# Moving mLSTM queries and keys into the seven-product stage of a hybrid decoder block, and DeltaNet key and value blocks in front of it

## The chip, the cores and the metric

One core of a Trainium2 chip runs the whole layer as one program. The metric is the device time of that program in microseconds (us), lower is better. A core has TensorE (PE in the profile; its weight loads are PEld), VectorE (DVE), ScalarE (ACT), GpSimd (POOL) and SyncE (SP), each of which works through its own list of instructions in order and waits on semaphores of the others. DMAs are issued from the lists of SP, ACT and POOL.

## What is computed

One decoder layer on 512 tokens, all in float32. A normalised input `u` (512 x 2048) is projected by one wide matrix, the columns go to two token mixers, and both results pass through one output matrix, sigmoid gates and a residual.

```python
def _hybrid_layer(h, norm_w, w_in, ...):
    u = _rmsnorm(h, norm_w)
    proj = jnp.matmul(u, w_in)
    (ml_q, ml_k, ml_v, ml_o, ml_z, ml_i, ml_f,
     dn_qkv, dn_z, dn_b, dn_a, gate_a, gate_b) = jnp.split(proj, idx, axis=-1)
    h_a = _mlstm_chunkwise(heads(ml_q), heads(ml_k), heads(ml_v), i_pre, logf)   # 8 heads
    h_a = merge(_rmsnorm(h_a)) * ml_norm_w * sigmoid(ml_o) * silu(ml_z)
    qkv = _causal_conv_silu(dn_qkv, dn_conv_w)          # 4 taps along the tokens, per channel
    dq, dk, dv = split(qkv)                             # 16 heads of 128 channels each
    h_b = _gated_delta_chunkwise(_l2norm(dq), _l2norm(dk), dv, beta, g)
    h_b = merge(_rmsnorm(h_b, dn_norm_w)) * silu(dn_z)
    return sigmoid(gate_a) * (h_a @ w_out[:2048]) + sigmoid(gate_b) * (h_b @ w_out[2048:])
```

The mLSTM has 8 heads with queries and keys of 128 channels (1024 columns of each in `w_in`); the DeltaNet has 16 heads of 128 channels for each of query, key and value.

## The kernel before

**Products.** Every float32 product is made of three TensorE products on values split in a high and a low part (`wh`/`wl` of the weights, `uh`/`ul` of the input): high by high, high by low, low by high. ACT makes the high part (`split_hi`, L140), DVE the low part (`split_lo`, L143). The order of TensorE's list is the order of the program text; the lists of the other engines are set by a scheduler that follows priorities (`urgent`, `high_priority`) and ties (`behind`, which puts an instruction after the newest split on an engine).

**Two ways to project.** `proj_cm` (L246) projects 256 columns straight: 16 row tiles x 2 column halves x 3 products = 96 matmuls of 128 x 512, and its result has channels on partitions and tokens along the row. Its weights come as tiles of 2 row tiles x 256 columns, four loads ahead (`load_raw`, a plan that lists every tile of the run) and three splits ahead. `seven_stage` (L480) projects two groups of 512 columns at once with a two-by-two scheme that needs seven block products where the straight way needs eight: 336 matmuls of 128 x 512 for 1024 columns, against 384. It costs extra sums on DVE (L519, L520, L538 on weights; L632 on results). A block has half A (8 stages of 4 products) and half B (8 stages of 3 products); the list `SEVEN` names the blocks, and each kind has a *sink* that takes the four results of a group off PSUM: `z` (gates of the mLSTM), `s` (gate of the DeltaNet), `q` (mLSTM queries and keys, turned to channels-first and written to DRAM), `v`, `g`.

**Stages.** (1) Front: the input is normalised, turned and split, while four `proj_cm` blocks run: queries and keys of mLSTM heads 0 to 3 (`QKFIRST = 2`), which `spill` writes to DRAM (`qk_d`). (2) The seven-product stage: 13 blocks; one of them is `q`, for heads 4 to 7. (3) Mixers: eight units (`dn_unit`), each for two DeltaNet heads. A unit runs three `proj_cm` blocks, key, value, query, and the rest of the work of several units and of the mLSTM heads is laid between their matmuls. (4) The output projection: three straight blocks, two seven-product blocks, one last straight block.

**Steps.** Work beside a projection is written as generators. `tick` (L219) is called after every six large matmuls (a *step*); a generator does a piece, says how many steps to wait, and goes on. So a unit of three `proj_cm` blocks has 48 steps, and the mixers have 384. For a unit, `conv_silu` and `silu_end` make convolution and SiLU (a scaled copy on ACT, three multiply-adds on DVE, tanh on ACT, one more on DVE), `turn` transposes 32 x 32 blocks on DVE and goes through DRAM for the rest. `dn_front_k` makes the products of the keys (`pk`), and solves small triangular systems on DVE (L964, L966) whose result comes back through DRAM as `tt` and is turned as `tn` (L982). `dn_back` (products `p1` to `p4`) starts 25 steps after the query block and needs `tn`. `dn_chain` runs through four chunks of tokens for each head: products `pr`, `pw`, `pst`, `po`, two steps apart, with one short DVE or ACT instruction between each (`r` L1082, `w` L1090, `st` L1100). `dn_front_q` makes `pqk` (L990), 9 steps after the query block. `ml_head` does the same for an mLSTM head (`psc`, `pnum`, `pcs`); `HEADS` lists the step at which each begins. All these short products share three PSUM buffers (`psw`) and the chains two (`pso`).

## Time and profile before

| | |
|---|---|
| time, median of 3 runs (lowest to highest) | 2144.73 us (2144.39 to 2144.76) |
| the profiled execution, its own time | 2143.23 us |
| its span in the profile | 2141.5 us |

The stages in the profiled execution (busy times of the engines inside each stretch, in us):

| stretch from the span's start | stage | length | PE | DVE | ACT | POOL |
|---|---|---|---|---|---|---|
| 0 to 124.6 | front | 124.6 | 107.93 | 89.10 | 59.45 | 5.15 |
| 124.6 to 1114.8 | seven-product stage, 13 blocks | 990.2 | 990.20 | 799.69 | 459.25 | 77.41 |
| 1114.8 to 1800.2 | mixers, 8 units | 685.4 | 685.10 | 557.43 | 383.61 | 276.39 |
| 1800.2 to 2141.5 | output projection | 341.3 | 330.28 | 261.77 | 155.34 | 92.17 |

How to read it: matmuls are pipelined, so one that takes 0.39 us on the page starts 0.23 us after the one before it; what a matmul costs is the distance between two starts, or the length of a stage divided by its matmuls. A busy PE means that the next matmul was always ready.

### The profile page before, as it was taken

The page shows a single profiled execution, that of the slowest core. Times are in us where ns is not written, and L with a number is a line of the kernel's source. Part 1 is how long each engine was busy: PE and PEld are TensorE (multiplying, and loading weights), DVE is VectorE, ACT ScalarE, POOL GpSimd, SP SyncE. Part 2 cuts the span into 40 slices and gives each one's busy share as a digit, 9 for nine tenths or more (in the row PEclk, how much of TensorE's full clock was granted, in tenths as well). Part 3 has the DMA queues.
Part 4 walks back from the last instruction along what each step waited for, and adds up shares of the span by engine and source line. Part 5 has one row for each costly group of instructions (what it writes and reads, how often), then busy time and mean ns, then how long its engine had stood idle before and what let it go on. Part 6 is the DMA issues. An engine that isn't in the chain of part 4 may idle for free.

```text
span 2141.5 us, 32018 instructions
## 1 busy us (share of the span) xinstructions
PE 2113.5 (99%) x10544; PEld 1752.6 (82%) x10544; DVE 1708.0 (80%) x2981; ACT 1057.6 (49%) x2066; POOL 451.1 (21%) x667
## 2 busy tenths in 40 slices
PE   6999999999999999999999999999999999999998
PEld 5888888888888888888888888888888888887886
DVE  5888888788788778777766887888878878569887
ACT  5444454445444444444445546456465464345345
POOL 0000000000004000000003335344343363233211
PEclk9999999999999999999999999999999999999999
DMA  5355676667677767766766867777686677778895
GB/s 162 119 192 190 212 217 198 220 199 224 206 234 237 245 196 226 240 209 212 253 205 165 208 166 180 183 180 192 182 211 173 171 189 224 196 223 287 245 302 225
DMA packets 447144, 444.21 MB, mean 207 GB/s; under 512 B 197121, under 2 KB 303842, under 8 KB 446850
## 3 DMA queue, kind: packets, MB, share of 16 engines
q1 hardware_dynamic: 377618, 337.22, 53.9%
q0 software_dynamic: 24752, 72.90, 10.9%
q10 hardware_dynamic: 44608, 32.06, 4.8%
q8 instruction: 82, 1.34, 0.3%
q14 instruction: 84, 0.69, 0.1%
HBM read 348.66 MB, written 97.58 MB: 208 GB/s over the span
## 4 chain that ended last, share of the span: by engine, by line
PE 95%; DVE 2%; DMA 2%; issue 1%; SPq 0%; POOL 0%; ACT 0%; DVEq 0%; POOLq 0%; ACTq 0%
PE ps L578 18%; PE ps L580 18%; PE ps L579 18%; PE pj L257 10%; PE pj L259 9%; PE pj L258 9%; PE py L1407 2%; PE py L1409 2%; PE py L1408 2%; PE pk L915 1%; DMA wr<-in_w_out_dram 1%; PE pqk L990 1%; PE pw L1087 1%; PE pnum L1213 1%; PE po L1102 1%
## 5 line engine op out<-in xcount | busy, mean ns | idle before, releaser
L143 DVE TENSOR_TENSOR wl<-wr,wh 128x512 fp32r<-128x512 f32 (+1 forms) x522 | 444.3, 852 | 176.5 <-ACT wh L140 172.3
L140 ACT CAST wh<-wr 128x512 fp32r<-128x512 f32 (+1 forms) x522 | 373.9, 717 | 422.1 <-PE pj L258 218.5
L257 PE MATMUL pj<-uh,wh 128*128 128x512 f32 x896 | 375.8, 419 | 0.0
L259 PE MATMUL pj<-uh,wl 128*128 128x512 f32 x896 | 351.5, 392 | 0.0
L258 PE MATMUL pj<-ul,wh 128*128 128x512 f32 x896 | 349.8, 390 | 0.0
L578 PE MATMUL ps<-wh,uh 128*128 128x512 f32 x752 | 292.7, 389 | 0.8 <-DVE X L632 0.8
L579 PE MATMUL ps<-wl,uh 128*128 128x512 f32 x752 | 292.6, 389 | 0.0
L580 PE MATMUL ps<-wh,ul 128*128 128x512 f32 x752 | 292.6, 389 | 0.0
L140 ACT CAST wh<-t 128x1024 fp32r<-128x1024 f32 x120 | 126.3, 1053 | 301.7 <-PE ps L580 197.5
L533 POOL DMA_DIRECT2D t_d<-ts x104 | 56.6, 544 | 921.8 <-DVE ts L520 853.5
L579 PE MATMUL ps<-wl,suh 128*128 128x512 f32 x624 | 242.9, 389 | 0.0
L580 PE MATMUL ps<-wh,sul 128*128 128x512 f32 x624 | 242.8, 389 | 0.0
L578 PE MATMUL ps<-wh,suh 128*128 128x512 f32 x624 | 242.8, 389 | 0.0
L140 ACT CAST wh<-ts 128x512 fp32r<-128x512 f32 x240 | 147.9, 616 | 184.7 <-DVE ts L538 157.6
L143 DVE TENSOR_TENSOR wl<-t,wh 128x1024 fp32r<-128x1024 f32 x120 | 147.0, 1225 | 81.9 <-ACT wh L140 81.5
L259 PEld LDWEIGHTS pj<-uh,wl 128*128 128x128 f32 x896 | 168.3, 188 | 37.0
L257 PEld LDWEIGHTS pj<-uh,wh 128*128 128x128 f32 x896 | 169.2, 189 | 29.7
L258 PEld LDWEIGHTS pj<-ul,wh 128*128 128x128 f32 x896 | 169.3, 189 | 28.5
L143 DVE TENSOR_TENSOR wl<-ts,wh 128x512 fp32r<-128x512 f32 x240 | 164.9, 687 | 32.6 <-ACT wh L140 31.2
L578 PEld LDWEIGHTS ps<-wh,uh 128*128 128x128 f32 x752 | 141.2, 188 | 30.4 <-DVE X L632 1.2
L579 PEld LDWEIGHTS ps<-wl,uh 128*128 128x128 f32 x752 | 141.2, 188 | 29.5
L580 PEld LDWEIGHTS ps<-wh,ul 128*128 128x128 f32 x752 | 141.2, 188 | 29.2
(345 smaller groups left out, 3804.2 us busy)
## 6 DMA issues: line engine op xcount, KB each, us to landing
wr<-in_w_in_dram SPq DMA_DIRECT2D x744, 256.0 KB, 3.6
wr<-in_w_out_dram SPq DMA_DIRECT2D x138, 256.0 KB, 4.8
t_d<-ts POOLq DMA_DIRECT2D x104, 256.0 KB, 3.6
wr<-t_d SPq DMA_DIRECT2D x104, 256.0 KB, 3.7
xt<-in_x_dram SPq DMA_DIRECT2D x8, 512.0 KB, 7.2
tg_d<-X ACTq DMA_DIRECT2D x16, 256.0 KB, 4.8
tg_d<-to ACTq DMA_DIRECT2D x16, 256.0 KB, 4.6
v<-v_d SPq DMA_DIRECT2D x8, 512.0 KB, 5.6
```

The lines of the kernel that those rows point to most:

```text
L140: newest["A"] = A.copy(hi, src).ins
L143: newest["V"] = V.tensor_tensor(out=lo, in0=src, in1=hi.bitcast(F32), op=ALU.subtract).ins
L257: T.matmul(ps[j], hi[:, k, wsl], uh[:, kt, :], start=(kt == 0), stop=False)
L258: T.matmul(ps[j], hi[:, k, wsl], ul[:, kt, :], start=False, stop=False)
L259: T.matmul(ps[j], lo[:, k, wsl], uh[:, kt, :], start=False, stop=(kt == KT - 1))
L533: queue.dma_start(t2_d[b % 2, i], ts[:, 0, :])
L578: T.matmul(ps[t], ah, hi, start=(g == "A" and i == 0), stop=False, skip_group_check=True)
L579: T.matmul(ps[t], ah, lo, start=False, stop=False, skip_group_check=True)
L580: T.matmul(ps[t], al, hi, start=False, stop=(i == KH - 1), skip_group_check=True)
L1407: T.matmul(ps[c], uh[:, kt, tsl], hi, start=(kt == ks[0]), stop=False)
L1408: T.matmul(ps[c], uh[:, kt, tsl], lo, start=False, stop=False)
L1409: T.matmul(ps[c], ul[:, kt, tsl], hi, start=False, stop=(kt == ks[-1]))
```

## The change

- **Columns change places.** All mLSTM queries and keys now go through the seven-product stage: `SEVEN` has two `q` blocks (one before the `v` blocks, one behind them), 14 blocks in all. The front's four `proj_cm` blocks are now DeltaNet blocks: the keys of heads 0 and 1, and the values of heads 3 and 5, 7 and 9, 11 and 13 (`PRE` lists their channel tiles). The value blocks load two column groups of 128 that lie 256 apart (kind `w`), in two DMAs per tile.
- **They are finished beside the stage.** `spill` writes the raw results to `raw_d`. In each of the first eight blocks of the seven-product stage, at the last stage of half A, `before_mixers` starts for one channel tile: load it, convolution and SiLU (one ACT multiply, three DVE multiply-adds, an ACT tanh, a DVE multiply-add), a DVE transpose, and the write to `pre_d` (for keys also to `kc_d`), issued from ACT.
- **Units get shorter.** Unit 0 has no key block (32 steps); units 1 to 6 project only one value head (`proj_half`: 48 matmuls, 8 steps; weight tiles of 4 row tiles x 128 columns) and load the other from `pre_d` (`turned`); they have 40 steps. Unit 7 keeps 48. The mixers have 320 steps.
- **Times within them.** `HEADS` is closer together, `dn_back` starts 28 steps after the query block (25 before; 27 in unit 0, 29 in unit 7 as before), and `dn_front_k` waits 11 steps for the solved systems in units 1 to 6 (16 before). `ml_head` loads keys and queries of all heads from `qt_d` and `k_d`; the transposes for heads 0 to 3 are gone. `open_y` starts at step 150 (200 before).

```diff
-QKFIRST = 2
-HEADS = (1, 41, 85, 130, 178, 226, 274, 322)
+HEADS = (1, 37, 74, 111, 148, 186, 225, 264)
+PRE = (16, 17, 35, 37, 39, 41, 43, 45)
+VPRE = {(h - 33) // 2: i for i, h in enumerate(PRE) if h > 32}
...
-         + [("q", ML_Q + QKS, ML_K + QKS)]
+         + [("q", ML_Q, ML_K)]
          + [("v", ML_V + c, ML_V + c + NO) for c in range(0, D, 2 * NO)]
+         + [("q", ML_Q + NO, ML_K + NO)]
...
-    QK = [(a, b) for b in range(QKFIRST) for a in range(2)]
-    plan = [("i", (ML_Q, ML_K)[a] + b * NB, k) for a, b in QK for k in range(0, KT, KP)]
+    FRONT = [("i", DN_K)] + [("w", DN_V + (h - 32) * P) for h in PRE[2::2]]
+    plan = [(*f, k) for f in FRONT for k in range(0, KT, KP)]
...
-        for c in (DN_K, DN_V, DN_Q):
-            plan += [("i", c + p * NB, k) for k in range(0, KT, KP)]
+        for c in (DN_K, DN_V, DN_Q)[p == 0:]:
+            if c == DN_V and p in VPRE:
+                plan += [("h", c + p * NB, k) for k in range(0, KT, 2 * KP)]
+            else:
+                plan += [("i", c + p * NB, k) for k in range(0, KT, KP)]
...
+    def proj_half(col0):
+        ps = psj.tile([P, S], F32, tag="pj", name="pj")
+        for kt0 in range(0, KT, 2 * KP):
+            hi, lo = next_w("h", col0, kt0)
+            for k in range(2 * KP):
+                kt = kt0 + k
+                T.matmul(ps, hi[:, k, :], uh[:, kt, :], start=(kt == 0), stop=False)
+                T.matmul(ps, hi[:, k, :], ul[:, kt, :], start=False, stop=False)
+                T.matmul(ps, lo[:, k, :], uh[:, kt, :], start=False, stop=(kt == KT - 1))
+                if k % 2:
+                    tick()
+        return [ps]
...
             for n in range(N - 2):
+                if n == KH - 1 and beside:
+                    start(beside.pop(0))
                 prep_sums(n0 + n + 1)
...
+    def before_mixers(i):
+        raw = wp.tile([P, S], F32, tag="wr", name="pr0", bufs=NRAW)
+        with behind("S"):
+            nc.sync.dma_start(raw, raw_d[i])
+        yield 4
+        ct = PRE[i]
+        y = wp.tile([P, S], F32, tag="wr", name="py0", bufs=NRAW)
+        with behind("A"):
+            A.mul(y, raw, convc[:, 144 + ct:145 + ct])
+        for j in (2, 1, 0):
+            with behind("V"):
+                V.scalar_tensor_tensor(out=y[:, 3 - j:S], in0=raw[:, 0:S - 3 + j], ...)
+            yield 1
+        with behind("A"):
+            A.activation(raw, y, AF.Tanh)
+        yield 1
+        with behind("V"):
+            V.scalar_tensor_tensor(out=y, in0=raw, scalar=1.0, in1=y, op0=ALU.add, op1=ALU.mult)
+        yield 1
+        with behind("V"):
+            V.transpose(raw, y)
...
-        yield 16
+        yield 11 if hs[0] // 2 in VPRE else 16
...
+            else:
+                nc.sync.dma_start(kq[j][:, 0, :], kc_d[j])
+                start(turned(ke, j), 3 + j, front)
...
-        ps = proj_cm(DN_V + dcol)
+        ps = (proj_half if p in VPRE else proj_cm)(DN_V + dcol)
...
-        start(dn_back(hs, kq, u), 25 + 4 * last, by)
+        start(dn_back(hs, kq, u), 28 - (p == 0) + last, by)
```

**Where it stands in DVE's list.** Two places show the order. The first is DVE in the second block of the seven-product stage, just behind the last two result sums of half A. `X` is the sum buffer, `wr3` a raw weight tile, `ts` a weight sum, `wl` a low part. Before:

```order
L632 TENSOR_TENSOR X_517<-X_517,ps_1806 128x512
L632 TENSOR_TENSOR X_517<-X_517,ps_1807 128x512
L143 TENSOR_TENSOR wl_2198<-wr3_2117,wh_2197 128x1024
L538 TENSOR_TENSOR ts_2223<-wr3_2155 128x512
L143 TENSOR_TENSOR wl_2230<-wr3_2155,wh_2229 128x1024
L538 TENSOR_TENSOR ts_2255<-wr3_2201 128x512
L143 TENSOR_TENSOR wl_2226<-ts_2223,wh_2225 128x512
L143 TENSOR_TENSOR wl_2258<-ts_2255,wh_2257 128x512
L143 TENSOR_TENSOR wl_2262<-wr3_2201,wh_2261 128x1024
```

In the changed kernel, at the same place (its lines are numbered anew: L632 is now L661, L143 is L146, L538 is L565; `py0` and `pr0` are the tiles of `before_mixers`):

```order
L661 TENSOR_TENSOR X_523<-X_523,ps_1847 128x512
L661 TENSOR_TENSOR X_523<-X_523,ps_1848 128x512
L146 TENSOR_TENSOR wl_2241<-wr3_2158,wh_2240 128x1024
L565 TENSOR_TENSOR ts_2271<-wr3_2196 128x512
L822 SCALAR_TENSOR_TENSOR py0_2254<-pr0_2208,convc_85,py0_2254 128x511
L146 TENSOR_TENSOR wl_2278<-wr3_2196,wh_2277 128x1024
L565 TENSOR_TENSOR ts_2307<-wr3_2244 128x512
L822 SCALAR_TENSOR_TENSOR py0_2254<-pr0_2208,convc_85,py0_2254 128x510
L146 TENSOR_TENSOR wl_2274<-ts_2271,wh_2273 128x512
L822 SCALAR_TENSOR_TENSOR py0_2254<-pr0_2208,convc_85,py0_2254 128x509
L146 TENSOR_TENSOR wl_2310<-ts_2307,wh_2309 128x512
L146 TENSOR_TENSOR wl_2314<-wr3_2244,wh_2313 128x1024
```

Three multiply-adds of the convolution (L822) now stand between the sums and low parts of the next three weight stages; the fourth and the transpose follow a few rows further down.

**Where it stands in TensorE's list.** The second place is PE in the mixers at `pqk` of unit 2 (`kq4`, `kq5`: keys and queries of heads 4 and 5). Before, it lies behind the last product `po` of the chains of unit 1, beside the first products of an mLSTM head (`pnum`, `pcs`):

```order
L1213 MATMUL pnum_12907<-v1_12723,wm_12539 128x257
L1102 MATMUL po_12430<-w_12872,aq_11079 128x128
L990 MATMUL pqk_12919<-kq4_11616 128x128 x4
L257 MATMUL pj_12710<-uh_89,wh_12755 128x512
L258 MATMUL pj_12710<-ul_90,wh_12755 128x512
L259 MATMUL pj_12710<-uh_89,wl_12756 128x512
L257 MATMUL pj_12710<-uh_89,wh_12755 128x512
L258 MATMUL pj_12710<-ul_90,wh_12755 128x512
L259 MATMUL pj_12710<-uh_89,wl_12756 128x512
L1219 MATMUL pcs_12937<-v1_12723,kw_12381 128x257
L990 MATMUL pqk_12947<-kq5_11617 128x128 x4
```

In the changed kernel it lies inside the chains of unit 1 (`pr` reads `kq2` and `kq3`, heads 2 and 3), and the mLSTM head has moved to other steps (L990 is now L1056, L1079 is L1145, L1084 is L1150, L257 to L259 are L284 to L286):

```order
L1145 MATMUL pr_13245<-st_13190,kq2_11192 128x128
L1150 MATMUL po_12983<-st_13190,kq2_11192 128x128
L1056 MATMUL pqk_13250<-kq4_12029 128x128 x4
L284 MATMUL pj_13022<-uh_91,wh_13073 128x512
L285 MATMUL pj_13022<-ul_92,wh_13073 128x512
L286 MATMUL pj_13022<-uh_91,wl_13074 128x512
L284 MATMUL pj_13022<-uh_91,wh_13073 128x512
L285 MATMUL pj_13022<-ul_92,wh_13073 128x512
L286 MATMUL pj_13022<-uh_91,wl_13074 128x512
L1145 MATMUL pr_13275<-st_13216,kq3_11193 128x128
L1150 MATMUL po_13001<-st_13216,kq3_11193 128x128
L1056 MATMUL pqk_13280<-kq5_12030 128x128 x4
```

The chain of one unit now runs through the `pqk` of the next: between the `pr` of one head and the `pr` of the other stand one `po`, the four products of `pqk` and one step of six large matmuls.

93 lines of the change are left out of this document (59 added, 34 removed).

## The prediction

> **What bounds the kernel now.** I read the page first, then the waits of PE, then the windows, one stage and one block or unit at a time.
>
> ```profile
> span 2141.5 us, 32018 instructions
> PE 2113.5 (99%) x10544; PEld 1752.6 (82%) x10544; DVE 1708.0 (80%) x2981; ACT 1057.6 (49%) x2066; POOL 451.1 (21%) x667
> ```
>
> PE is busy in 99% of the span and no other engine in more than 80%. A busy PE could still be one that waits in small pieces, so the waits of PE come next; the columns are engine, line, what it waited for, us in total, times, longest.
>
> ```profile
> PE pprm L108 <- POOL rs L304: 14.6, 1, 14.6
> PE put L313 <- DVE xt L290: 2.1, 2, 1.3
> PE ps L578 <- DVE X L632: 0.8, 1, 0.8
> PE ps L578 <- DVE X L1431: 0.7, 2, 0.5
> PE pw L1087 <- DVE r L1082: 0.3, 1, 0.3
> ```
>
> That is the whole list. The first two are the start, L632 and L1431 lie in the output projection. In the seven-product stage and the mixers together, 1675 us, PE waits once, for 0.3 us. So between 20 us and 1900 us the time is the number of matmuls times the distance between two starts, and the question is what the change does to that number, and whether the engines behind it keep up.
>
> The windows (stretch, then busy us and instruction counts of PE, PEld, DVE, ACT, POOL, clock, DMA share, GB/s): the seven-product stage, three of its blocks (a `z`, the `q`, the last `g`), and one unit of the mixers from one `pk` to the next.
>
> ```profile
> 124.60:1114.80 990.20, 990.20 (x4369) 819.81 (x4368) 799.69 (x1018) 459.25 (x653) 77.41 (x143) 1.00 0.68 217
> 200.80:277.00 76.20, 76.20 (x338) 63.11 (x337) 63.89 (x84) 36.40 (x54) 4.31 (x8) 1.00 0.64 207
> 581.60:657.80 76.20, 76.20 (x338) 63.08 (x337) 64.24 (x84) 35.11 (x52) 7.79 (x14) 1.00 0.69 224
> 1038.60:1114.80 76.20, 76.20 (x338) 63.11 (x337) 55.63 (x71) 34.81 (x51) 5.15 (x16) 1.00 0.66 219
> 1399.60:1485.50 85.90, 85.90 (x531) 71.91 (x530) 70.51 (x178) 48.19 (x135) 36.16 (x49) 1.00 0.73 184
> ```
>
> The reader is to see three things. 13 blocks of 336 matmuls are 4368, so one costs 990.20 / 4368 = 0.2267 us and a block 76.2 us. A block costs 76.2 us whatever its sink: DVE has 63.9 us of work in the `z` block, 64.2 in the `q`, 55.6 in the `g`, and PE's time is the same. And a unit is 85.9 us with DVE at 70.5, or 82%.
>
> In the mixers the large matmuls start a little further apart:
>
> ```profile
> 1396.01 0.39 PE L257 MATMUL pj<-uh,wh 128*128 128x512 f32 x1
> ...
> 1398.98 0.39 PE L258 MATMUL pj<-ul,wh 128*128 128x512 f32 x1
> ```
>
> The second is the 13th after the first, so 2.97 / 13 = 0.2285 us.
>
> **The change part by part: PE.** Removed: unit 0's key block, 96 matmuls, and half a value block, 48, in each of units 1 to 6, together 384. At 0.2285 that is 87.7 us, at 0.2267 it is 87.1. Added: one block, 336 x 0.2267 = 76.2 us. The front keeps four blocks of 96. The short products are all still there. Net 48 large matmuls fewer: 10.9 to 11.5 us, and I take **11.2**. A unit of 40 steps should then take 85.9 - 48 x 0.2285 = 74.9 us.
>
> [...]
>
> **The work that goes beside the seven-product stage.** It is priced from the same instructions where they stand now, in the mixers (line, engine, operation, tiles, shapes, count; then busy us, mean ns; then idle before and its cause):
>
> ```profile
> L143 DVE TENSOR_TENSOR wl<-wr,wh 128x512 fp32r<-128x512 f32 x24 | 18.9, 789 | 6.9 <-ACT wh L140 6.7
> L837 DVE SCALAR_TENSOR_TENSOR vt<-yp,convc,vt 128x512 f32<-128x512 f32 x6 | 4.5, 768 | 0.0
> L844 DVE SCALAR_TENSOR_TENSOR vt<-th,vt 128x512 f32<-128x512 f32 x16 | 10.9, 679 | 0.0
> L860 DVE STREAM_TRANSPOSE to<-vt 128x512 f32<-128x512 f32 x16 | 11.2, 702 | 1.8 <-DMA td<-to 1.8
> L835 ACT ACTIVATE vt<-yp,convc 128x512 f32<-128x512 f32 x16 | 11.6, 724 | 0.5
> L843 ACT ACTIVATE th<-vt 128x512 f32<-128x512 f32 x16 | 10.1, 629 | 6.0 <-DVE vt L837 6.0
> ```
>
> DVE gets 3 x 0.768 + 0.679 + 0.702 = 3.7 us for each of eight blocks, ACT 0.72 + 0.63 = 1.4. The fullest of the three blocks goes from 64.2 to 67.9 us of DVE in 76.2. It starts at the end of half A, where the sums of half A (L632) fall, and runs through half B, which needs fewer weight sums. Below, it costs nothing; above, if all of it stood in PE's way, 8 x 3.7 = 30 us. I take 0, since the 8.6 us between the `g` and the `q` block already cost nothing; what is uncovered is only the part beyond DVE's 12 us of idle time.
>
> The ACT multiply is a new wait: it needs the load of `raw_d`, and the casts of the next weight stage stand behind it on ACT, DVE's low parts behind those, and PE behind them. The load is issued four steps ahead, 24 x 0.2267 = 5.4 us, and loads of this size land in this time:
>
> ```profile
> wr<-in_w_in_dram SPq DMA_DIRECT2D x744, 256.0 KB, 3.6
> gz<-gz_d SPq DMA_DIRECT2D x16, 256.0 KB, 4.2
> mkq<-qk_d SPq DMA_DIRECT2D x8, 256.0 KB, 5.7
> ```
>
> At worst 0.3 us late in eight blocks, 2.4 us; ACT idles half of each block, so I take 0. The half-width weight tiles have rows of 128 values like `gz`, 4.2 us against 3.6. In the mixers ACT waits before its casts for PE to free a split buffer, not for the load, so 0.6 us more costs 0:
>
> ```profile
> L140 ACT CAST wh<-wr 128x512 fp32r<-128x512 f32 x24 | 14.8, 617 | 26.1 <-PE pj L258 22.7 <-PE pj L259 3.4
> ```
>
> The front's value tiles take two DMAs on SP instead of one; there too the tiles are four ahead, 0. The writes of `pre_d` take the place of as many issues on SP in the mixers, now on ACT. The second `q` block adds 16 issues to POOL; the first did not lengthen its block, 0.
>
> **Shorter units.** DVE loses per unit four splits and one head's SiLU: 4 x 0.789 + 3.7 = 6.9 us. So 63.6 us in 74.9, 85% for 82%. `dn_front_k` waits five steps less for the solved systems. Now (start, length, engine):
>
> ```profile
> 1379.96 0.36 SPq L979 DMA_DIRECT2D tt<-xd  x1
> 1383.98 2.07 POOL L1012 COPY tb<-tt 32x256 f32<-32x256 f32 x4 [2.16 <-DMA tt<-xd]
> 1397.93 0.43 DVE L982 STREAM_TRANSPOSE tn<-tt 128x256 f32<-128x256 f32 x1
> ```
>
> `tt` is there at 1383.98 and used at 1397.93: 14 us to spare. Five steps of 74.9 / 40 = 1.87 us are 9.4, so some 4.6 stay: 0. Unit 0 needs its keys 8 steps after the start, 10.9 us, against 5.7 for a load like `mkq`: 0. Unit 6's chains end three steps later against the end of the mixers, at most 4 us and only if they are late; unit 7, which ends last, keeps its times: 0.
>
> What I do charge is the chains: `pr` and `pqk` of two units now take turns in the three PSUM buffers, with DVE fuller. The one wait of this kind in the list above is 0.3 us; one for most of the six short units makes **1.5**; the bounds are 0, and what the first rival gives. Nothing here makes the chains faster, but the waits of the output projection (0.8 + 0.7) could also vanish, 1.5 the other way.
>
> **Sum.** 2143.23 - 11.2 + 1.5 = 2133.5 for a profiled execution. The median of the runs is 1.5 above it (2144.73), so **2135.0**.
>
> **The rivals.** (1) *The chains give it back.* Each short unit waits twice at the crossing of `pr` and `pqk`, each time as long as PE's longest wait on DVE now, 0.8 us: 12 x 0.8 = 9.6, and the time is 2144.7 - 11.2 + 9.6 = 2143.1. For it: the crossing is new, and DVE is in order. Against: the same engines wait only once now, and between `pr` and the next use of its buffer lies a step of 1.4 us and `pqk`.
>
> (2) *DVE becomes the bound of the mixers: slower.* DVE idles 85.9 - 70.5 = 15.4 us per unit. If that is not spare but forced (waits on ACT's casts, on PE, on loads), it stays, and a unit takes 63.6 + 15.4 = 79.0 instead of 74.9: 6 x 4.1 = 25 us, the time 2144.7 - 11.2 + 25 = 2158. It decides from 11.2 / 6 = 1.9 us of waiting per unit, when forced idle is above 13.2 us. For it: splits wait 6.9 us per unit on ACT. Against: ACT itself waits there for PE (22.7 us, above), so this idle shrinks with PE's time.
>
> (3) *The added work is in the way* of the seven-product stage, in part: 1 us in each of eight blocks leaves 2143. I count it with (1).
>
> **How the numbers follow.** My forecast has 0.75; rivals (1) and (3) together 0.15, of which a third stays under the bound below; rival (2) 0.10. A change within 0.2%, 4.3 us, can hardly be told from none here. So faster 0.80, same 0.10, slower 0.10. The range starts at 2131.5 (11.5 off, and the output waits gone) and reaches to 2142, into (1) and (3).
>
> **What would show it.** PE: 14 blocks of 76.2 us from 124.6 to 1191.4; six units of 74.9; a list of PE waits still under 3 us beside the start. If a unit is longer, the row of waits names it: `pr`, `pw` or `pqk` on DVE is (1); many on `wl` with DVE near 100% is (2). If a block with `before_mixers` exceeds 76.2, it is (3). I am wrong if PE's waits add up to 7 us.

## The result and the profile after

| | before | after |
|---|---|---|
| time, median (lowest to highest), 4 runs each | 2144.56 us (2143.84 to 2144.76) | 2175.99 us (2174.85 to 2177.24) |
| ratio, 95% interval | | 1.0144 (1.0131 to 1.0156) |
| the profiled execution, its own time | 2143.23 us | 2174.87 us |

The change makes the kernel 31 us slower. The forecast was 2135.0 us, the range ended at 2142. The first two lines of the page of the changed kernel:

```profile
span 2173.1 us, 32187 instructions
PE 2118.9 (98%) x10496; PEld 1749.3 (80%) x10496; DVE 1747.9 (80%) x3027; ACT 1061.9 (49%) x2072; POOL 465.1 (21%) x707
```

PE is busy for 5 us more than before, with 48 matmuls fewer, and idle for 54 us of the span instead of 28. The windows by stage say where (stretch, length, then busy us of PE, PEld, DVE, ACT, POOL, granted clock, DMA share, GB/s): seven-product stage, mixers up to the first `py`, output projection.

```profile
124.56:1191.18 1066.62, 1066.56 (x4705) 882.79 (x4705) 887.66 (x1140) 499.70 (x712) 102.65 (x182) 1.00 0.70 223
1191.18:1812.51 621.33, 597.04 (x3609) 494.17 (x3609) 492.06 (x1263) 339.21 (x960) 260.51 (x374) 0.98 0.72 181
1812.51:2173.10 360.59, 347.54 (x1673) 284.52 (x1671) 279.20 (x454) 163.62 (x303) 96.75 (x133) 0.99 0.78 243
```

The same stretch of the mixers in the kernel before, cut at the first `py` too:

```profile
1114.84:1785.66 670.82, 670.52 (x4003) 560.91 (x4002) 543.02 (x1352) 375.19 (x1012) 272.49 (x374) 1.00 0.74 186
```

The seven-product stage is as forecast: 14 blocks in 1066.62 us, 76.19 each. The mixers should have become 384 x 0.2285 = 87.7 us shorter, 583.1 us. They take 621.3, so **38.2 us are lost there**: PE is idle for 621.33 - 597.04 = 24.3, and busy for 597.04 - 583.1 = 13.9 longer than the same matmuls took. The output projection takes 360.6 us instead of 355.8. DVE's idle time in the mixers is 670.82 - 543.02 = 127.8 us before and 621.33 - 492.06 = 129.3 after: DVE got 51 us less to do in a stage that was to be 88 us shorter, and its idle time did not shrink at all.

The waits of PE in the changed kernel (line, what it waited for, us in total, times, longest), beside the start's:

```profile
PE pr L1145 <- DVE st L1164: 6.0, 3, 2.4
PE p L1086 <- DVE tn L1048: 3.1, 1, 3.1
PE pj L286 <- DVE wl L146: 2.6, 1, 2.6
PE p L1113 <- ACT tb L1108: 2.6, 2, 1.5
PE p L1101 <- ACT s L1091: 2.4, 4, 1.1
...
PE pw L1153 <- DVE r L1148: 1.9, 1, 1.9
PE pst L1160 <- DVE tmp L1030: 1.4, 1, 1.4
```

No single wait explains the loss: the chains (`pr`, `pw`, `pst`), the products behind the solve (`p`), and a weight split each give a few us. One unit cut into eighths, from one `pk` to the next, shows what stands behind several of them. Before (the busy time of DVE is the third in the row of PE, PEld, DVE, ACT, POOL):

```profile
1313.60:1324.32 10.72, 10.72 (x130) 8.79 (x129) 8.69 (x33) 7.37 (x22) 6.31 (x10) 1.00 0.78 220
1324.32:1335.05 10.73, 10.73 (x73) 8.46 (x72) 7.79 (x12) 8.03 (x21) 7.57 (x10) 1.00 0.53 127
1335.05:1345.78 10.73, 10.73 (x59) 9.17 (x58) 8.58 (x21) 3.08 (x8) 2.68 (x5) 1.00 1.03 248
1345.78:1356.50 10.72, 10.72 (x63) 9.32 (x62) 9.97 (x36) 4.36 (x11) 2.64 (x3) 1.00 0.86 228
1356.50:1367.22 10.72, 10.72 (x59) 9.15 (x58) 10.55 (x30) 4.39 (x9) 0.00 (x0) 1.00 0.31 85
1367.22:1377.95 10.73, 10.73 (x61) 9.30 (x60) 9.35 (x29) 7.60 (x29) 4.74 (x6) 1.00 0.63 145
1377.95:1388.68 10.73, 10.73 (x49) 8.95 (x48) 7.41 (x10) 4.54 (x10) 7.46 (x15) 1.00 0.90 227
1388.68:1399.40 10.72, 10.72 (x49) 8.87 (x48) 9.00 (x18) 9.46 (x33) 3.61 (x5) 1.00 0.67 130
```

And after:

```profile
1282.20:1292.26 10.06, 10.06 (x82) 8.18 (x81) 8.27 (x23) 9.95 (x27) 4.71 (x12) 1.00 1.00 230
1292.26:1302.33 10.07, 10.07 (x103) 8.02 (x102) 6.32 (x20) 6.87 (x22) 4.72 (x4) 1.00 0.72 186
1302.33:1312.39 10.06, 10.06 (x60) 8.17 (x60) 4.57 (x8) 4.64 (x14) 1.71 (x3) 1.00 0.64 166
1312.39:1322.45 10.06, 10.06 (x55) 8.60 (x54) 9.83 (x30) 5.25 (x13) 3.31 (x4) 1.00 0.64 184
1322.45:1332.51 10.06, 10.06 (x59) 8.72 (x58) 9.82 (x25) 2.04 (x4) 3.24 (x6) 1.00 0.65 160
1332.51:1342.58 10.07, 8.66 (x50) 7.23 (x49) 9.79 (x20) 3.16 (x9) 6.98 (x11) 1.00 0.74 165
1342.58:1352.64 10.06, 8.19 (x38) 6.71 (x38) 9.65 (x29) 3.75 (x8) 4.92 (x8) 0.83 0.68 200
1352.64:1362.70 10.06, 10.06 (x48) 8.36 (x47) 9.65 (x21) 8.73 (x38) 4.62 (x4) 1.00 0.49 108
```

Before, DVE is full in one eighth (10.55 of 10.72 us) and has a little room in all others. After, it is full in five eighths on end (96 to 98%), and idles for almost half of the two before them (6.32 and 4.57 of 10.07). This is the fullest unit: in the next two, three eighths on end reach 94 to 98% and four reach 95 to 99%; in the next unit of the kernel before it is again one (10.57 of 10.74). In the full stretch lie the solve, the chains, the query block's convolution and the next unit's key convolution; in the other `p1` to `p4`, the value block and most of an mLSTM head. PE's waits in this unit stand late in the full stretch; in the next two units they stand in the first to third eighth, just behind the full stretch of the unit before.

A part of the 13.9 us lies in stretches behind waits in which PE runs at a granted clock of 0.50, here from 1373.06 to 1379.89 us (start, length, engine, what it waited for):

```profile
1370.41 0.39 PE L286 MATMUL pj<-uh,wl 128*128 128x512 f32 x1
1373.88 1.06 PE L1086 MATMUL p<-tn,aq 32*32 32x32 f32 x32 [3.08 <-DVE tn L1048]
...
1375.89 0.63 PE L286 MATMUL pj<-uh,wl 128*128 128x512 f32 x1
1376.32 0.63 PE L284 MATMUL pj<-uh,wh 128*128 128x512 f32 x1
1376.74 0.63 PE L285 MATMUL pj<-ul,wh 128*128 128x512 f32 x1
```

Behind the wait of 3.08 us the large matmuls start 0.43 us apart, not 0.23. There are four such stretches in the mixers, near 1350, 1376, 1630 and 1726 us, some 20 us long together, so about 10 of the 13.9 us. The kernel before has none there. Where the other 4 us lie was not traced.

### The profile page after: what moved, and what is told of

It reads as the page before. It is cut to its first block, busy times and chain, and to the rows that moved or that the text cites. A ratio compares the mean times of both kernels' runs of the same rounds, so it can differ in the third digit from the quotient of the medians.

```text
span 2173.1 us, 32187 instructions
## 1 busy us (share of the span) xinstructions
PE 2118.9 (98%) x10496; PEld 1749.3 (80%) x10496; DVE 1747.9 (80%) x3027; ACT 1061.9 (49%) x2072; POOL 465.1 (21%) x707
## 4 chain that ended last, share of the span: by engine, by line
PE 75%; DMA 8%; DVE 7%; issue 5%; ACT 2%; POOL 1%; SPq 1%; ACTq 0%; DVEq 0%; POOLq 0%
PE ps L606 17%; PE ps L607 17%; PE ps L605 17%; PE pj L284 5%; PE pj L286 5%; PE pj L285 5%; DMA y_d<-ty 1%; PE py L1480 1%; PE py L1481 1%; PE py L1482 1%; DVE wl L146 1%; DMA wr<-in_w_out_dram 1%; DVE xi L1032 1%; DVE tmp L1030 1%; DVE kq L903 1%
## 5 line engine op out<-in xcount | busy, mean ns | idle before, releaser
L146 DVE TENSOR_TENSOR wl<-wr,wh 128x512 fp32r<-128x512 f32 (+1 forms) x506 | 427.6, 846 | 158.8 <-ACT wh L143 150.9
L143 ACT CAST wh<-wr 128x512 fp32r<-128x512 f32 (+1 forms) x506 | 367.5, 727 | 372.1 <-PE pj L285 120.4
L605 PE MATMUL ps<-wh,uh 128*128 128x512 f32 x800 | 311.4, 389 | 0.8 <-DVE X L661 0.8
L606 PE MATMUL ps<-wl,uh 128*128 128x512 f32 x800 | 311.5, 389 | 0.2
L607 PE MATMUL ps<-wh,ul 128*128 128x512 f32 x800 | 311.3, 389 | 0.0
L143 ACT CAST wh<-t 128x1024 fp32r<-128x1024 f32 x128 | 134.8, 1053 | 319.2 <-PE ps L607 212.1
L284 PE MATMUL pj<-uh,wh 128*128 128x512 f32 x672 | 285.6, 425 | 0.8 <-ACT yp L894 0.8
L286 PE MATMUL pj<-uh,wl 128*128 128x512 f32 x672 | 265.7, 395 | 2.6 <-DVE wl L146 2.6
L285 PE MATMUL pj<-ul,wh 128*128 128x512 f32 x672 | 263.9, 393 | 0.0
L606 PE MATMUL ps<-wl,suh 128*128 128x512 f32 x672 | 261.5, 389 | 0.1
L143 ACT CAST wh<-ts 128x512 fp32r<-128x512 f32 x256 | 158.1, 618 | 183.5 <-DVE ts L565 154.1
L146 DVE TENSOR_TENSOR wl<-t,wh 128x1024 fp32r<-128x1024 f32 x128 | 156.6, 1224 | 82.8 <-ACT wh L143 82.3
L146 DVE TENSOR_TENSOR wl<-ts,wh 128x512 fp32r<-128x512 f32 x256 | 175.2, 685 | 24.0 <-ACT wh L143 22.5
L546 DVE TENSOR_TENSOR t<-wr 128x1024 f32<-128x1024 f32 x128 | 156.0, 1219 | 8.5 <-DMA wr<-in_w_in_dram 4.8
L286 PEld LDWEIGHTS pj<-uh,wl 128*128 128x128 f32 x672 | 127.2, 189 | 31.6 <-DVE wl L146 3.0
L606 PEld LDWEIGHTS ps<-wl,suh 128*128 128x128 f32 x672 | 126.1, 188 | 26.7 <-DVE wl L146 0.5
```

Of the source, the lines that this page charges most:

```text
L143: newest["A"] = A.copy(hi, src).ins
L146: newest["V"] = V.tensor_tensor(out=lo, in0=src, in1=hi.bitcast(F32), op=ALU.subtract).ins
L284: T.matmul(ps[j], hi[:, k, wsl], uh[:, kt, :], start=(kt == 0), stop=False)
L285: T.matmul(ps[j], hi[:, k, wsl], ul[:, kt, :], start=False, stop=False)
L286: T.matmul(ps[j], lo[:, k, wsl], uh[:, kt, :], start=False, stop=(kt == KT - 1))
L546: V.tensor_tensor(out=t13, in0=r[:, 1:3, :], in1=r[:, 0:2, :], op=ALU.subtract)
```

## The experiments

Every time is a median; beside it stands the gap to the kernel before in the same comparison (for the changed kernel +31.4 us). *Lost* is the length of the mixers in the profiled execution over the sum of their matmuls as forecast (583.1 us, with the matmuls that an edit adds or takes), and its part in which PE is idle. The profiled execution is one of those behind the median and can lie up to 7 us from it: for e17 it is the slowest of five, 2169.83 us, so its 29.8 are too many beside its median.

| run | edit of the changed kernel | time | gap | ratio, 95% interval | lost (idle) |
|---|---|---|---|---|---|
| (changed kernel) | | 2175.99 | +31.4 | 1.0131 to 1.0156 | 38.2 (24.3) |
| e1 | `pqk` behind the chain | 2167.73 | +20.8 | 1.0082 to 1.0115 | 31.0 (23.3) |
| e2 | no queries by decay on GpSimd | 2174.24 | +27.3 | 1.0110 to 1.0140 | 36.9 (22.5) |
| e3 | two taps left out | 2159.64 | +12.7 | 1.0041 to 1.0071 | 22.6 (13.8) |
| e4 | 96 matmuls fewer | 2184.57 | +37.6 | 1.0152 to 1.0191 | 71.0 (52.1) |
| e5 | solve in 10 steps | 2182.25 | +36.1 | 1.0151 to 1.0186 | 39.2 (23.3) |
| e6 | key links urgent | 2174.94 | +28.8 | 1.0117 to 1.0151 | 38.6 (25.6) |
| e7 | e5 and e1 | 2178.77 | +32.6 | 1.0139 to 1.0169 | 39.6 (25.6) |
| e8 | kernel before, five stalls | 2167.94 | +21.8 | 1.0091 to 1.0121 | |
| e9 | 96 matmuls more | 2181.65 | +36.0 | 1.0154 to 1.0184 | 22.6 (13.9) |
| e10 | no convolution on DVE | 2152.48 | +6.8 | 1.0021 to 1.0043 | 17.0 (10.5) |
| e11 | no GpSimd multiplies | 2167.09 | +21.4 | 1.0088 to 1.0119 | 32.6 (22.2) |
| e12 | 288 matmuls more | 2217.46 | +71.8 | 1.0318 to 1.0352 | 14.6 (9.4) |
| e13 | no query convolution on DVE | 2145.68 | -0.2 | 0.9992 to 1.0011 | 9.7 (8.2) |
| e14 | no value convolution, no norms | 2169.35 | +23.5 | 1.0096 to 1.0129 | 33.8 (23.1) |
| e15 | unit 0 six steps later | 2189.00 | +43.1 | 1.0180 to 1.0212 | 50.7 (36.4) |
| e16 | queries finished early, not values | 2160.10 | +14.2 | 1.0050 to 1.0080 | 22.0 (15.9) |
| e17 | e16 and e1 | 2162.56 | +17.4 | 1.0069 to 1.0097 | 29.8 (19.1) |
| e18 | e17, clears later | 2163.69 | +18.5 | 1.0067 to 1.0094 | 23.7 (15.6) |

The first question was whether the waits come from the new order (A: `pqk` and chains cross), from GpSimd (B), from DVE's load (C), or from a floor of the short units that PE does not set.

### e1: `pqk` behind the chain

```diff
-QWAIT = 9
+QWAIT = 20
```

> The products pqk, with the DVE multiply and the two GpSimd multiplies behind them, go from the 9th step after the query block (inside the chain of the unit before: steps 79 to 99 of a unit, pqk at 89) to the 20th, behind the chain, as they lay in the kernel before. Theory A (the crossing of pqk with pr, pw and pst makes the chain's links late): PE's waits at pr, pw and pst (9.3 us in the changed kernel) and about half of the stretches at half clock go, 12 to 18 us in all: 2158 to 2164 us. Theory B (GpSimd multiplies hold up DVE wherever they lie) and theory C (DVE has too much to do in 40 steps): the waits move to other places, 2170 to 2180 us.

10.6 us came back, fewer than A asked for, and PE's idle time hardly fell (24.3 to 23.3): the waits at `pr`, `pw` and `pst` went from 9.3 to 5.4 us, and others came at `pk` and `pcs`.

### e2: without the multiply of the queries on GpSimd

```diff
-            G.tensor_tensor(out=qt, in0=qt, in1=eg, op=ALU.mult)
```

> Leaves out the GpSimd multiply of the queries by the decay row (qt *= eg, two of 128 x 512 per unit). DVE instructions that overlapped it took 16.4 us longer than usual in the mixers of the changed kernel, against 2.6 us in the kernel before. Theory B (GpSimd holds up DVE): DVE's excess falls by about 14 us and PE's waits with it, with the half-clock stretches 15 to 22 us less: 2154 to 2161 us. Theory A (the place of pqk's matmuls and of their DVE multiply): 2172 to 2178 us. Theory C (DVE's load): these are not DVE's instructions, 2170 to 2176 us.

4 us. That multiply is not the cause, though a DVE instruction beside two of these multiplies took 3.93 us instead of 0.24 (last section).

### e3: one tap of the convolution

```diff
         A.mul(dst, yp[:, 3:S + 3], convc[:, 144 + ct:145 + ct])
-        for j in (2, 1, 0):
+        for j in (2,):
```

> Leaves out two of the three multiply-adds of the convolution in the mixers, 10 per short unit, 7.7 us of DVE per unit, at an unchanged order of the steps. Theory C (DVE's load in 40 steps): nearly all waits go, mixers 585 to 592 us instead of 621: 2140 to 2148 us. Theory A or B (the order, or GpSimd, makes single links late whatever the load): the chain's waits stay, at most a third goes: 2162 to 2172 us.

18.7 us, the largest so far, and less than mean load promised.

### e4 and e9: fewer and more matmuls in the half value blocks

```diff
e4:
-                T.matmul(ps, lo[:, k, :], uh[:, kt, :], start=False, stop=(kt == KT - 1))
e9:
+                T.matmul(ps, lo[:, k, :], uh[:, kt, :], start=False, stop=False)
                 T.matmul(ps, lo[:, k, :], uh[:, kt, :], start=False, stop=(kt == KT - 1))
```

> Leaves out the third product (low part of the weights) of the half value blocks: 16 matmuls in each of the six short units, 96 x 0.2285 = 21.9 us of PE, with the same steps and the same work on every other engine. If PE still bounds the units and the waits are local: 2176 - 21.9 = 2154 us. If the units have a floor on other engines (rival 2 of the prediction: idle time of DVE that is forced stays): the time saved comes back as waits, 2168 to 2176 us.

> Issues the third product (low part of the weights) of the half value blocks twice: 16 matmuls more in each of the six short units, 21.9 us of PE in all, everything else and the order of every other list as in the changed kernel. If the short units stand at a floor that other engines set (forced idle time of DVE, rival 2), the added matmuls fill waits: 2172 to 2180 us, as without them. If PE bounds the units and the waits are tied to the order of the lists: 2176 + 21.9 = 2198 us.

With 21.9 us of PE work less the kernel is 6 us slower than with all of it, with 21.9 us more it is 5 us slower. So **PE's work no longer sets the short units**. In e4 most of the time comes back in one place. PE's idle time in the mixers grows from 24.3 to 52.1 us, and this wait, the largest of its list, from 3.1 to 26.1:

```profile
PE p L1085 <- DVE tn L1047: 26.1, 3, 11.3
```

`tn` is the turned result of the solve. In e9 the added matmuls fill what were waits: the loss falls from 38.2 to 22.6 us.

### e5, e6 and e7: is the path to `tn` too long?

In the changed kernel the solve takes 43 to 47 us in units 1 to 3, against 32 to 36 before, and its result is sent for (`tt`) 82 to 87 us after `pk`, against 66 to 70. `tn` waits for it in DVE's list, in front of the next unit's key work:

```profile
DVE tmp L1030 <- DMA ls<-ld: 14.4, 5, 4.5
...
DVE tn L1048 <- DMA tt<-xd: 5.7, 3, 2.7
```

The first wait, for the solve's input, was 5.9 us before (3.7 more at the same line are put down to another transfer), and there was none on `tt`. Theory S says that this path sets the unit.

```diff
e5:
-            if i % 2:
+            if i % 3 == 2:
                 yield 1
e6:
+        with urgent():
             V.tensor_scalar(out=nk, in0=nk, scalar1=EPS, scalar2=None, op0=ALU.add)
             V.reciprocal(cs, nk)
...
-            with behind("A"):
+            with urgent():
                 for c in range(NC):
                     if j:
e7: e5 and QWAIT = 20
```

> The 31 rounds of the triangular solve are laid over 10 steps instead of 15 (three rounds per step, not two), all else as in the changed kernel. There the solve's result tt comes 82 to 87 us after the unit's pk in units 1 to 4, against 66 to 70 us in the kernel before, and tn, which turns it, stands in DVE's list among the key work of the next unit. Theory S (the path from pk over the solve to tn has become too long for its 40 steps, and a late tn holds up the next unit's keys): tt comes at most 78 us after pk, the waits on tn (5.7 us of DVE, 3.1 us of PE) go and part of the others with them: 2156 to 2166 us. Theories A and C (crossing of the chains; DVE's load): the solve only crowds other places, 2172 to 2182 us.

> The short instructions between pk and the solve's first transfer (nk, cs on DVE, the scaling of aq on ACT) get the priority that the chain's instructions have, at the same steps. From pk to the last issue of ld are 24 us in the changed kernel and 16.5 us in the kernel before. Theory S (see the run with the solve in 10 steps): these go to 17 to 20 us, DVE's waits on ls (14.4 us) shrink, 2160 to 2168 us. If these links are late because DVE's list in front of them is too full (theory C), priority changes little: 2170 to 2180 us.

> The solve in 10 steps together with pqk behind the chain (20th step). The second alone gave 2167.7 us. If late solves (S) and the crossing (A) are two causes, their gains add: 2148 to 2158 us. If they are the same waits seen twice: 2162 to 2168 us. If neither place matters but only DVE's load (C): 2166 to 2176 us.

S falls in this form. Asking for the solve in fewer steps does not make it shorter (43 to 45 us in units 1 to 3), and priority changes 3 us. e7 also shows how far e1's gain can be trusted: with the solve in 10 steps the same edit brings 3.5 us. Differences under some 10 us between kernels whose lists were reordered are not read as causes below.

### e8: stalls in the kernel before

```diff
+    def stall(n):
+        pa = psw.tile([P, P], F32, tag="wk", name="sa")
+        T.matmul(pa, ident, ident, start=True, stop=True)
+        y = wk.tile([P, P], F32, tag="w", name="sy")
+        with urgent(3):
+            for _ in range(n):
+                A.copy(y, pa)
+        pb = psw.tile([P, P], F32, tag="wk", name="sb")
+        T.matmul(pb, ident, y, start=True, stop=True)
...
+    for s, n in ((68, 2), (116, 5), (164, 8), (212, 11), (260, 16)):
+        start(stall(n), s, "B")
```

> The kernel before, with five stalls of PE put into the mixers, 48 steps apart: a product, 2, 5, 8, 11 or 16 copies of its result on ACT one behind the other, and a product that needs the last copy. At 0.25 to 0.3 us a copy they are estimated at 1.2, 2.0, 2.8, 3.6 and 5 us, 14.5 us in all. Theory D (a wait of 2 to 3 us halves the granted clock for the next 3 to 7 us): the longer three or four are followed by such stretches, and the time grows by 6 to 12 us more than the stalls: 2165 to 2172 us. Without it the stalls cost their own length: 2157 to 2161 us.

The five stalls delayed the next matmul by 0.41, 1.30, 2.25, 3.15 and 4.64 us, 11.8 in all, and the kernel became 21.8 us slower. In the clock of the trace, 3.4 us behind the third stall and 6.8 behind the fifth are at half clock, which makes up 5.1 us of the rest; where the other 5 us lie was not traced. In the trace of the changed kernel the granted clock changes only at borders of intervals of 3.41 us (last section). Windows of this run on such intervals: the one with the third stall and the one behind it, then the two in which the fourth stall lies and the one behind them (clock third from the end):

```profile
1397.89:1401.31 3.42, 1.11 (x6) 0.76 (x4) 2.39 (x4) 2.55 (x10) 0.00 (x0) 1.00 0.49 108
1401.31:1404.72 3.41, 3.22 (x9) 2.64 (x10) 0.00 (x0) 2.37 (x12) 0.00 (x0) 0.50 0.67 142
1490.05:1493.47 3.42, 1.49 (x8) 1.10 (x6) 2.77 (x5) 2.16 (x8) 0.00 (x0) 1.00 0.44 109
1493.47:1496.88 3.41, 1.94 (x9) 1.65 (x10) 0.00 (x0) 2.61 (x12) 0.00 (x0) 1.00 0.73 146
1496.88:1500.29 3.41, 3.41 (x16) 2.82 (x15) 0.79 (x5) 3.22 (x16) 1.20 (x2) 1.00 0.73 215
```

D holds, with a correction: the stall of 2.25 us was followed by slow matmuls, the longer one of 3.15 us was not. So length alone did not decide. The two also differ in place: the shorter stall lies almost whole in one interval and leaves PE idle for 2.31 of its 3.42 us, the longer one is split over two, 1.93 and 1.47 us.

### e10 and e11: no convolution, no GpSimd multiplies

```diff
e10:
-        for j in (2, 1, 0):
-            V.scalar_tensor_tensor(out=dst, in0=yp[:, j:j + S], ...)
...
-        V.scalar_tensor_tensor(out=dst, in0=th, scalar=1.0, in1=dst, op0=ALU.add, op1=ALU.mult)
e11:
-            G.tensor_tensor(out=dm, in0=dm, in1=bc(cs[:, j, :], P), op=ALU.mult)
-            G.tensor_tensor(out=ke, ...)
-            G.tensor_tensor(out=qt, in0=qt, in1=eg, op=ALU.mult)
-        G.tensor_tensor(out=g, in0=g, in1=bc(rsd, P), op=ALU.mult)
-        G.tensor_tensor(out=qi, in0=qi, in1=iwb, op=ALU.mult)
-            G.tensor_tensor(out=g[i], in0=g[i], in1=bc(sm, P), op=ALU.mult)
```

> Leaves out the convolution's three multiply-adds and SiLU's last one in the mixers: 4 DVE instructions for each of 5 channel tiles per short unit, 14.9 us of DVE's 63.6 per unit. Theory C (DVE's load): DVE falls to 65% of a unit, the waits go, the mixers come down from 621 to 583 to 590 us: 2135 to 2143 us. If the waits come from the order of the lists and from transfers, whatever DVE's load: 2152 to 2162 us.

> Leaves out all six kinds of GpSimd's 128 x 512 multiplies in the mixers (queries by decay, keys by decay, dm by cs, and the three that scale gates and mLSTM queries). Theory B (GpSimd stretches DVE: 54.4 us beyond usual durations in the mixers of the changed kernel): DVE gets about 40 us of its time back, like a cut of its load by 5 us per unit, and 2150 to 2162 us. If DVE's stretched instructions are seldom those PE waits for: 2168 to 2176 us.

e10 brought 24.6 us, where mean load asked for 33 to 41; its units 2 to 6 take 75 to 77 us, close to the forecast 74.9, and the rest of its loss is in unit 0 and near the end. In e11 DVE's busy time in the mixers falls by 39 us, from 492 to 453, and the time by only 10. Its list of PE's waits is another one than that of the changed kernel:

```profile
PE p L1085 <- DVE tn L1048: 18.0, 3, 8.9
...
PE pr L1144 <- DVE st L1163: 0.7, 1, 0.7
```

The waits at `pr`, `pw` and `pst` are almost gone (1.2 us, 9.3 in the changed kernel), but PE waits 18.0 us for `tn` (3.1 there), behind the solves of units 1 to 3. These take 43 to 46 us as in the changed kernel, though DVE has less to do. Why they stay long is open, so e11 does not settle how large a part GpSimd has (B).

### e12: 48 matmuls more in each short unit

```diff
                 T.matmul(ps, hi[:, k, :], uh[:, kt, :], start=(kt == 0), stop=False)
                 T.matmul(ps, hi[:, k, :], ul[:, kt, :], start=False, stop=False)
+                T.matmul(ps, lo[:, k, :], uh[:, kt, :], start=False, stop=False)
+                T.matmul(ps, hi[:, k, :], uh[:, kt, :], start=False, stop=False)
+                T.matmul(ps, hi[:, k, :], ul[:, kt, :], start=False, stop=False)
                 T.matmul(ps, lo[:, k, :], uh[:, kt, :], start=False, stop=(kt == KT - 1))
```

> Issues all three products of the half value blocks twice: 48 matmuls more in each short unit, 65.8 us of PE in all, so that a unit has PE work for 85.9 us as in the kernel before, but DVE's load and the places of the steps of the changed kernel. If the waits are those of too little PE time per unit (floor near 79 us), they all go, and the half clock with them: 2176 + 65.8 - 38 = 2204 us (2200 to 2208). If the new places of the steps make the waits (theory A), at least half stay: 2222 to 2242 us.

Between the two: of 38 us lost, 24 go when a unit has PE work for 86 us, and 15 stay; that they belong to the new places of the steps is argued, not shown.

### e13 and e14: the same DVE work taken from the one part and from the other

The eighths above gave the next theory, F: what counts is DVE's load in the part of the unit in which it is full. (The expectations call the two parts halves.)

```diff
e13, in the query block:
-            conv_silu(ps[j], hs[j], kq[j][:, 1, :], yp=yq[j])
+            conv_silu(ps[j], hs[j], kq[j][:, 1, :], yp=yq[j], taps=())
e14, in the value block, and in dn_front_k:
-            conv_silu(ps[j], 32 + hs[j], vt.rearrange("p c t -> p (c t)"))
+            conv_silu(ps[j], 32 + hs[j], vt.rearrange("p c t -> p (c t)"), taps=())
...
-                for c in range(NC):
-                    V.scalar_tensor_tensor(out=jk, in0=aq[:, c, 0, :], ..., accum_out=nk[:, j, c:c + 1])
+        G.memset(nk, 1.0e6)
```

In both, SiLU's last multiply-add of that block is left out too.

> Leaves out DVE's part of convolution and SiLU for the queries only: 8 instructions, 6.0 us per short unit, all in the half of the unit in which DVE is busy 95 to 100% of the time (from about 40 us after pk to the next pk). Theory F (DVE is full in that half and idles in the other, so that the mean of 82% says nothing): 15 to 22 us less, 2153 to 2160 us, as much as two taps of all blocks (7.7 us per unit) brought. Mean load (theory C as first put): in proportion to the run without any convolution (14.9 us per unit, 24 us less), about 10 us: 2164 to 2168 us.

> Leaves out as much DVE work of the other half: convolution and SiLU of the values (3.0 us per short unit) and the eight short sums jd that make the keys' norms (3.0 us; the norms are a constant). DVE is busy 33 to 80% there. Theory F: 0 to 7 us less, 2168 to 2176 us. Mean load: about 10 us less, 2164 to 2168 us. If the path from pk to the solve sets the unit (theory S), the sums stand on it: 2158 to 2165 us.

The mixers of e13, e14 and e16 (below), in this order:

```profile
1191.50:1784.30 592.80, 584.58 (x3609) 487.12 (x3608) 457.18 (x1207) 338.49 (x959) 257.89 (x374) 1.00 0.75 189
1192.30:1809.20 616.90, 593.85 (x3609) 492.75 (x3609) 458.70 (x1103) 338.92 (x959) 262.21 (x383) 0.99 0.73 183
1192.60:1797.70 605.10, 589.19 (x3609) 486.98 (x3609) 495.41 (x1263) 338.56 (x960) 257.25 (x374) 1.00 0.75 188
```

This is the pair that decides. e13 gave more than F had asked for; e14 lies in F's range, though only 1 us above the one of mean load, so it is the distance of 24 us between the two that tells. DVE is busy for 457.2 and 458.7 us, the same; the mixers take 592.8 and 616.9. Against the changed kernel, with DVE's busy time 35 us shorter in the full part the mixers become 28.5 us shorter, with 33 us less in the other part 4.4.

The second figure is likely too low: e14's edit also adds a clear to GpSimd's list and brings its work on `nk` forward at the start of unit 0, and this unit takes 58.8 us (53.9 in the changed kernel), with two PE waits of 3.9 and 2.4 us. Behind unit 0, e13 gains 30.0 us for 35 us of DVE time, e14 9.3 us for 29. So work in the full part counts about three times as much, and work in the other part is not free.

In e13 the short units 2 to 6 (from the first projection matmul of one to that of the next) take 74.8 to 76.2 us, the forecast length, the solve takes 28 to 34 us in units 1 to 6, `tt` is sent for after 63 to 67 us, and PE's clock is 1.00. In e14 the solve still takes 43 to 48 us in units 1 to 3. So the long solve of theory S goes when the query block's DVE work goes: it is an effect of what stands beside it in DVE's list, and itself a link that PE can wait for (`tn` in e4 and e11).

### e16: queries instead of values

```diff
-PRE = (16, 17, 35, 37, 39, 41, 43, 45)
-VPRE = {(h - 33) // 2: i for i, h in enumerate(PRE) if h > 32}
+PRE = (16, 17, 3, 5, 7, 9, 11, 13)
+QPRE = {h // 2: i for i, h in enumerate(PRE) if h < 16}
...
-        ps = (proj_half if p in VPRE else proj_cm)(DN_V + dcol)
+        ps = proj_cm(DN_V + dcol)
...
-        ps = proj_cm(DN_Q + dcol)
+        ps = (proj_half if p in QPRE else proj_cm)(DN_Q + dcol)
...
+            if j == len(ps):
+                nc.sync.dma_start(kq[j][:, 1, :], kc_d[QPRE[p]])
+                start(turned(qn, QPRE[p]), 6, front)
```

> The same number of blocks and steps, but the six heads that are projected in front and finished beside the seven-product stage are queries instead of values: a short unit has full key and value blocks and half a query block. DVE's 3.7 us for that head leave the full half of the unit and 3.7 us for a value come into the half in which it idles; DVE's sum per unit is the same. Theory F: 8 to 15 us less, 2161 to 2168 us. Mean load: no change, 2172 to 2178 us.

The edit leaves nothing out, DVE is busy for 3 us more in the mixers (495.4), and 17.2 of the 31.4 us come back; the time lies 1 us below F's range. Units 2 to 4 take 75 to 76 us, the solve 32 to 36 us in units 1 to 6. It is the best complete version that was tried, and 14 us slower than the kernel before (1.0050 to 1.0080).

One part of F's picture does not hold: the full eighths are still there. The unit of the mixers that begins near 1360 us has four eighths on end at 93 to 95% in e16, and eighths of 95 and 96% in e13, and PE does not wait there. One row of each, e16 first:

```profile
1408.00:1417.49 9.49, 9.49 (x62) 8.44 (x61) 9.04 (x19) 1.67 (x4) 6.79 (x8) 1.00 0.83 247
1416.29:1425.80 9.51, 9.51 (x53) 8.02 (x52) 9.10 (x29) 4.33 (x8) 1.76 (x3) 1.00 0.43 113
```

A full eighth says where DVE's work is worth taking away; whether PE waits behind it may depend also on how much is queued there, which no row shows.

### e15, e17 and e18: what is left

The mixers of e13 and e16 still lose 10 and 22 us, 3 to 5 of them in unit 0 (55.4 and 54.0 us, where 72.5 - 96 x 0.2285 = 50.6 were due). There DVE waits 7.6 us for `dm`, the decay rows, whose load stands in GpSimd's list behind two clears (start, length, idle before and its cause; changed kernel):

```profile
1201.94 0.96 POOL L877 MEMSET tb<- 128x1024 f32 x1 [8.75 <-DMA wr<-in_w_in_dram]
1202.83 0.53 POOL L879 MEMSET ta<- 64x512 f32 x1
1203.30 1.07 POOL L884 DMA_DIRECT2D gb<-rows_d  x2
...
1208.95 1.41 POOL L953 TENSOR_SCALAR_AFFINE_SELECT dm<-gb 128x512 f32<-128x512 f32 x2 [3.60 <-DMA gb<-rows_d]
```

```diff
e15:
-        start(dn_front_k(hs, kq, u), 1, front)
+        start(dn_front_k(hs, kq, u), 1 if p else 7, front)
...
-        yield 11 if hs[0] // 2 in VPRE else 16
+        yield 16 if hs[0] // 2 == UNITS[-1] else 11
e17: e16 and QWAIT = 20
e18: e17, and
-    G.memset(tb, 0.0)
-    G.memset(ta, 0.0)
...
+        if hs[0] == 0:
+            G.memset(tb, 0.0)
+            G.memset(ta, 0.0)
```

> Unit 0's key work starts 6 steps later (pk at step 14 instead of 8), and its wait for the solved systems is 11 steps instead of 16. In the changed kernel DVE stands 7.6 us there before its first product of keys, for the decay rows dm, whose load GpSimd can only issue 12 us after the mixers begin; PE waits 3.8 us behind it and 6 us at half clock follow. If that is the cause: 6 to 8 us less, 2168 to 2170 us. If DVE is late there for other work: 2174 to 2178 us.

> Queries instead of values finished beside the stage (2160.1 us alone), and pqk behind the chain (20th step; 2167.7 us alone, against 2176). Theory F: pqk's two DVE multiplies (1.4 us) leave the full half for its end; both edits relieve the same half, so the gains do not add in full: 2152 to 2158 us. If pqk's place mattered for itself (theory A), the gains add: 2148 to 2153 us. If it was chance of the order: 2158 to 2164 us.

> The same kernel, and GpSimd's two clears of tb and ta, in front of unit 0's row loads in its list, stand in front of their first use instead. With query halves PE still waits 4.6 us in unit 0 behind the 7.6 us for which DVE stands before the first aq. If the clears, which wait for the space of a weight tile, hold up the rows: PE's waits in unit 0 go, 4 to 6 us less than the run before. If the row loads wait for that space themselves: no change (within 1.5 us).

e15 misses: the waits at unit 0's start go, but its solve then takes 45 us instead of 34, PE waits 8.4 us for `tn`, and the kernel is 12 us slower than the changed one. (Its expectation puts half clock behind that wait; the profiled execution of the changed kernel shows none there, that of e9 does, 1229.0 to 1232.4 us.) e17 misses too: with query halves, `pqk` behind the chain brings nothing, so neither its place (A) nor F's account of it is shown; the expectation's third case, chance of the order, is the one whose range holds the 2162.56 us. e18 answers its question: without the clears in front, GpSimd stands at the row load itself until 1203.4 us, for the same weight tile's space; the wait before the first `aq` is 6.7 us (8.0 in e17), the time the same within its scatter.

## Why the prediction was wrong, point by point

- **48 matmuls fewer, 11.2 us; a block 76.2 us; the seven-product stage ends at 1191.4.** Right: 14 blocks, end at 1191.18, and a unit can take 75 us (e13, which leaves out the query convolution).
- **The added work beside that stage: 0.** Right. All blocks are 76.2 us (one 76.5), DVE 887.66 of 1066.62 us. Rival (3) did not happen.
- **DVE's 63.6 us in 74.9, 85%, priced at 0.** This is the step that failed: I took DVE's 15.4 us of idle time per unit for room. The sum was right, by the row of units 1 to 6:

```profile
1245.30:1716.00 470.70, 455.31 (x2824) 376.81 (x2823) 382.50 (x971) 257.57 (x745) 204.56 (x296) 0.98 0.73 182
```

  382.50 / 6 = 63.8 us of DVE per unit, in 470.70 / 6 = 78.5. But I read 82% and 85% as room everywhere, from one window of a whole unit. By eighths DVE had one full already; the change took eight steps of PE and one value head's DVE work out of the light part, and left the DVE work of the query block and of the next key block, which lies in the heavy one, as it was. What stood in place of the 0: mixers of 621.3 us for 583.1, with PE idle for 24.3. e13 against e14 shows that DVE's work in the heavy part counts about three times as much as in the other, e16 that taking one head's work from there and putting another's into the light part is worth 17 us.
- **Rival (2), DVE becomes the bound: 10%, a unit of 79.0 us, 2158.** Its price per unit agrees with the mean (78.5, with 14.7 us of idle DVE per unit against 15.4), and its sign was right. The agreement is in part luck: single units take 69.4 to 85.7 us, and the time that it gave, 2158, is 18 us too low. I argued it away with "this idle shrinks with PE's time". It did not: 127.8 us before, 129.3 after. The wait that I had named, of DVE's low parts for ACT's high parts, fell only with the number of splits, from 58.8 us for 193 to 49.1 for 161, 0.30 us each both times, though ACT's own wait for PE behind it fell from 188.3 to 89.6 us. Others grew: for the solve's input (`ls`, 14.4 us, was 5.9), for `dm` in unit 0 (7.6, new) and for `tt` (5.7, new).
- **`tt` and `tn`: 14 us to spare, 9.4 used, 4.6 stay.** Wrong in size: I took the length of the solve from the kernel before. It grew by 7 to 11 us in units 1 to 4 and `tt` came 15 to 21 us later, so the spare time was negative: DVE waited 5.7 us for it and PE 3.1.
- **Unit 0's keys are there in time: 0.** The keys were, `dm` was not. I had counted the key load and not the decay rows in GpSimd's list. PE has two waits there, 0.8 and 2.6 us. That `dm` makes them is not shown: in e15 they go with a later start, but the kernel gets slower.
- **Crossing of `pr` and `pqk`: 1.5, rival (1) 9.6.** PE's waits at `pr`, `pw` and `pst` came to 9.3 us, as rival (1) had it. But putting the crossing right brings between -3 and 11 us (e17, e7, e1), so it is not shown to be the cause.
- **What no step had:** waits that cost more than their length (in e8, 21.8 us for 11.8 us of stalls). Of the 38.2 us, 13.9 are busy PE, about 10 of it lost at half clock. I had charged waits at their own length.
- **Output projection: unchanged or 1.5 less.** It took 4.8 us more (360.6 against 355.8), of which 1.9 are new waits on its first splits. Not followed further.
- **"I am wrong if PE's waits add up to 7 us":** those in the mixers add up to 24.

What stays open: some 10 us or more that every version loses (e13 9.7, e12 14.6), why the solve stays long in e11, and how far the waits at `pr` depend on the order that the scheduler happens to make.

## What to carry to other kernels

When PE is shortened in one part of a loop, look at the other engines in slices of that loop, not at their mean: here DVE was at 82%, but most of the room was in the part from which work was taken. Take from the slices that are full, and if the choice is free (values or queries here) let the slices decide it; then measure, since a full slice does not yet say that the bound engine waits (in e16 four eighths at 93 to 95% had no wait of PE). And test a claim of spare time by adding or removing work of one engine at equal order: 96 matmuls more or fewer made a difference of 5 to 6 us in the same direction, which says in two runs that PE had ceased to be the bound.
